# A two-layer decoder trunk: the last chunk before each FFN by token halves, ordered weight splits in the down projections, and buffers of their own for the z halves

## The chip, the core and the metric

The program runs on one core of one Trainium2 chip, whose engines work side by side, each through its own queue in order: PE does the matrix products, ACT (ScalarE) and DVE (VectorE) the element-wise work and the emptying of PSUM, POOL and SP issue transfers. The metric is the time of one execution in microseconds on the device. It is a median over a few runs.

## The reference

The trunk takes 1024 tokens of width 1024 through a gated short-convolution layer and an attention layer with a compressed K/V, each followed by a SwiGLU FFN of inner width 2816. All is float32. Cut to its core:

```
def swiglu_ffn(h, w13, w2):
    g, u = split(h @ w13, 2)
    return (silu(g) * u) @ w2
h = h + short_conv_mixer(rms_norm(h, g0), w_in, conv_w, w_out)   # (gate_b * conv(gate_c * val)) @ w_out
h = h + swiglu_ffn(rms_norm(h, g1), w13, w2)
k_nope, k_pe, v = shared_mla_kv(h, ...)
h = h + mla_mixer(rms_norm(h, g2), ..., w_o, k_nope, k_pe, v)    # causal attention, then @ w_o
h = h + swiglu_ffn(rms_norm(h, g3), w13, w2)
return rms_norm(h, g4)
```

## The kernel before

Activations lie transposed, 128 channels by 1024 tokens, and the tokens are handled as two halves T1 and T2 of 512. Every operand of a product, weight or activation, is split into a high part (a rounding cast on ACT, L95) and a low part (the rest, a subtraction on DVE, L96), and PE multiplies three times: high by high, high by low, low by high.

Most of the work runs in `pair` (L147 to L188). A pair of output blocks for two token halves and two halves of the inner dimension is made from seven products instead of eight (a Strassen form). The products are named "1" to "7" and run in the order SEQ = 1, 5, 6, 2, 7, 3, 4, but 1, 5, 6, 3, 7, 2, 4 (SEQ0) for the first pair of an FFN. Each has its own combination of weight blocks (made by DVE at L158 to L168, into a raw buffer `sums` or in place) and of activations (made by `operands`, L252). A product is 12 matmuls where the inner dimension has four chunks of 256. Products 1, 6, 7 and 4 add up in one and the same PSUM bank Z (`ps_z`), so each of these must wait until the value before it has been copied or added out; 5 and 3 add up in the bank Y (`ps_y`), and 2 has a bank beside it. In `blocks` (up projections and the conv input) the values after 1, 5 and 6 are copied by ACT into half tiles `z1`, `z5`, `z6` (L197), and DVE adds them to later products (L237). Six half tiles (tag "half", L73) serve z1, z5, z6, `u2` and the activation sums `t` together.

The FFN's down projection is `back` (L477 to L519). It takes the inner dimension in four groups of two, three, three and three chunks, and in each group four pairs of output blocks; a product is 6 matmuls in the first group, 9 in the others. Its results are collected in `h`: in the first group ACT copies four of the seven (L501) and DVE adds the others, later DVE adds all (L503). In the third group the residual stream is fetched again (`hs`, L515). Weights come through ten raw buffers (`wraw`) and five split buffers (`wop`).

Before each FFN stand the projections conv_out (`classic`, L213, two chunks of 128 channels at a time, 48 matmuls each) and w_o (`project_o`, L1017). When two chunks are done, `final` (L540) scales them by the gain on ACT (`xg`, L544), makes the seven activation operands, and queues the squares for the norm (`stats`, L296 on ACT, L297 on DVE). What stands in `queue` is put out between the products by `drip`.

The order in which each engine sees its instructions is decided by a scheduler at build time, from the order in the code and a modelled timeline; `sums` of a later pair can so come before evictions of an earlier one.

## Time and profile before

| | |
|---|---|
| runs | 2120.62, 2125.85, 2125.18 us; median 2125.18 us |
| profiled execution | 2121.5 us, its span 2119.7 us, mean granted TensorE clock 0.994 |
| PE | busy 2077.5 us (98% of the span), 9798 matmuls |
| PE's weight loads | 1730.1 us (82%) |
| DVE | 1627.7 us (77%), 2694 instructions |
| ACT | 935.5 us (44%) |
| POOL | 245.2 us (12%) |
| DMA | 321.28 MB, mean 152 GB/s |

Busy time of PE covers pipelined matmuls that overlap, so PE's idle stretches have to be looked for one by one. Times in rows of the trace count from the start of the span.

### The profile page before, as it was taken

The numbers are of one execution on the slowest core, as the hardware profiler recorded it, in microseconds if no ns is written. First come the engines' busy times: TensorE is split into PE (matmuls) and PEld (weight loads), VectorE is DVE, ScalarE is ACT, GpSimd is POOL, SyncE is SP. The second block draws the span as 40 slices with busy tenths as digits, with TensorE's granted clock in tenths as the row PEclk, the third lists the DMA queues.
The fourth block names the chain that finished last, engine by engine and source line by source line (L and its number), as shares of the span: only waits on it lengthen the run. The fifth ranks groups of instructions, "written<-read, shape, count | busy, mean of one in ns | idle before, by whom it ended". The sixth has DMA issues, their size and how long they took to land.

```text
span 2119.7 us, 27634 instructions
## 1 busy us (share of the span) xinstructions
PE 2077.5 (98%) x9798; PEld 1730.1 (82%) x9798; DVE 1627.7 (77%) x2694; ACT 935.5 (44%) x1729; POOL 245.2 (12%) x464
## 2 busy tenths in 40 slices
PE   8999999999999999999999999999999999999998
PEld 6878887888888878888888888887888888878886
DVE  5697757789988887689467767767888888887785
ACT  6633344444444453224345545445444444443235
POOL 1000100000101121110002022100001010121100
PEclk9999999999999999999999999999999999999998
DMA  6133462343545587865222124522445445685851
GB/s 246 35 96 119 145 208 92 122 147 127 179 139 168 178 305 236 272 220 156 62 52 68 38 63 124 170 82 85 128 134 175 141 159 154 199 285 195 292 186 80
DMA packets 266858, 321.28 MB, mean 152 GB/s; under 512 B 19343, under 2 KB 214096, under 8 KB 266720
## 3 DMA queue, kind: packets, MB, share of 16 engines
q0 software_dynamic: 61248, 201.46, 28.1%
q1 hardware_dynamic: 205472, 118.07, 19.0%
q8 instruction: 77, 1.26, 0.2%
q14 instruction: 61, 0.50, 0.1%
HBM read 206.22 MB, written 108.00 MB: 148 GB/s over the span
## 4 chain that ended last, share of the span: by engine, by line
PE 88%; DVE 6%; DMA 2%; ACT 2%; issue 2%; SPq 0%; POOL 0%; POOLq 0%; ACTq 0%; DVEq 0%
PE ps_z L183 35%; PE ps_y L183 26%; PE ps_c L228 7%; PE ps_s L947 4%; PE ps_wo L108 1%; PE ps_wo L110 1%; PE ps_wo L112 1%; PE ps_l L112 1%; PE ps_l L108 1%; PE ps_l L110 1%; PE ps_pv L985 1%; PE ps_pv L986 1%; DMA w<-in_conv_ffn_w_dram 1%; PE ps_pv L987 1%; PE ps_q L108 1%
## 5 line engine op out<-in xcount | busy, mean ns | idle before, releaser
L183 PE MATMUL ps_z<-x,wo 128*128 128x512 f32 x2532 | 608.7, 389 | 3.6 <-ACT z L197 2.8
L183 PEld LDWEIGHTS ps_z<-x,wo 128*128 128x128 f32 x2532 | 474.6, 188 | 104.4 <-ACT z L197 4.1
L183 PE MATMUL ps_y<-x,wo 128*128 128x512 f32 x1764 | 432.3, 389 | 1.2 <-DVE x L96 0.9
L183 PEld LDWEIGHTS ps_y<-x,wo 128*128 128x128 f32 x1764 | 330.5, 188 | 70.9 <-DVE x L96 1.8
L95 ACT CAST wo<-w 128x512 fp32r<-128x512 f32 (+2 forms) x423 | 238.7, 570 | 278.0 <-PE ps_z L183 109.0
L96 DVE TENSOR_TENSOR wo<-w,wo 128x512 fp32r<-128x512 f32 (+2 forms) x423 | 260.4, 622 | 61.9 <-ACT wo L95 61.0
L183 PE MATMUL ps_z<-xm,wo 128*128 128x512 f32 x960 | 239.0, 392 | 4.2 <-ACT wo L95 1.6
L183 PEld LDWEIGHTS ps_z<-xm,wo 128*128 128x128 f32 x960 | 178.6, 188 | 46.3 <-DVE h L503 3.4
L95 ACT CAST wo<-sums 128x512 fp32r<-128x512 f32 (+2 forms) x172 | 98.3, 572 | 256.7 <-PE ps_y L183 101.5
L183 PE MATMUL ps_y<-xm,wo 128*128 128x512 f32 x720 | 181.6, 390 | 2.0 <-DVE h L503 2.0
L88 POOL DMA_DIRECT2D md<-x x140 | 74.9, 536 | 737.8 <-DVE x L96 704.8
L183 PEld LDWEIGHTS ps_y<-xm,wo 128*128 128x128 f32 x720 | 134.7, 188 | 31.0 <-DVE h L503 2.9
L197 ACT COPY z<-ps_z 128x512 f32<-128x512 f32 x106 | 62.0, 585 | 136.6 <-PE ps_z L183 136.5
L96 DVE TENSOR_TENSOR wo<-sums,wo 128x512 fp32r<-128x512 f32 (+2 forms) x172 | 107.2, 623 | 14.3 <-ACT wo L95 12.7
L88 POOL DMA_DIRECT2D xm<-md x140 | 74.1, 535 | 251.3 <-PE ps_z L183 126.3
L503 DVE TENSOR_TENSOR h<-ps_z,h 128x512 f32<-128x512 f32 x104 | 71.4, 687 | 36.5 <-PE ps_z L183 35.7
L96 DVE TENSOR_TENSOR x<-t,x 128x512 fp32r<-128x512 f32 x136 | 92.0, 684 | 5.1 <-ACT x L95 5.1
L237 DVE TENSOR_TENSOR a<-ps_y,z 128x512 f32<-128x512 f32 x88 | 60.6, 688 | 42.4 <-PE ps_y L183 42.1
L95 ACT CAST x<-t 128x512 fp32r<-128x512 f32 x136 | 82.4, 621 | 20.9 <-DVE t L252 20.3
L953 ACT ACTIVATE p<-ps_s,mx,qscale 128x128 f32<-128x128 f32 (+3 forms) x64 | 53.4, 835 | 82.4 <-DVE mx L951 80.0
L158 DVE TENSOR_TENSOR sums<-w,w 128x512 f32<-128x512 f32 (+2 forms) x85 | 53.2, 626 | 29.4 <-DMA w<-in_mla_ffn_w_dram 13.4
L503 DVE TENSOR_TENSOR h<-ps_y,h 128x512 f32<-128x512 f32 x88 | 60.2, 685 | 19.9 <-PE ps_y L183 19.8
(297 smaller groups left out, 3344.8 us busy)
## 6 DMA issues: line engine op xcount, KB each, us to landing
md<-x POOLq DMA_DIRECT2D x140, 512.0 KB, 3.6
xm<-md POOLq DMA_DIRECT2D x140, 512.0 KB, 8.1
w<-in_conv_ffn_w_dram SPq DMA_DIRECT2D x88, 256.0 KB, 2.8
w<-in_mla_ffn_w_dram SPq DMA_DIRECT2D x88, 256.0 KB, 3.0
w<-in_conv_w_in_dram SPq DMA_DIRECT2D x48, 256.0 KB, 3.0
hd<-h POOLq DMA_DIRECT2D x24, 512.0 KB, 3.6
w<-in_conv_ffn_w_dram SPq DMA_DIRECT2D x48, 192.0 KB, 4.9
w<-in_mla_ffn_w_dram SPq DMA_DIRECT2D x48, 192.0 KB, 4.5
```

What stands on the lines that cost most here:

```text
L88: nc.gpsimd.dma_start(dst, src)
L95: nc.scalar.copy(out=hi, in_=src)
L96: (eng or nc.vector).tensor_tensor(lo, src, hi.bitcast(F32), ALU.subtract)
L108: nc.tensor.matmul(ps[:, hs], lhsT=wh, rhs=xh(k)[:, hs], start=st, stop=False)
L158: tt(sums, R["12"], R["22"], ALU.add)
L183: mm = lambda w_, x_, f: nc.tensor.matmul(b, lhsT=w_[:, m], rhs=x_, start=f, stop=True, skip_group_check=True)
L197: nc.scalar.copy(out=kept[name], in_=b)
L228: nc.tensor.matmul(ps[:, ts], lhsT=w_[:, m], rhs=X[i][f"b{kh}{th}"][:, q, :], start=st and j == 0, stop=en and j == 2)
L237: nc.vector.tensor_tensor(dst, ps, add, ALU.add)
L503: nc.vector.tensor_tensor(dst[name], b, dst[name], ALU.add)
L947: nc.tensor.matmul(ps[:, a:b], lhsT=q[:, qs], rhs=k[:, a:b], start=i == 0, stop=i == 4 and b < kw)
L953: nc.scalar.activation(p, ps[:, :kw], AF.Exp, bias=mx, scale=qscale[:, qb:qb + 1], accum_out=rsum)
```

## The change

Token halves. The last of the eight 128-channel chunks of conv_out, and of w_o, does all matmuls for T2 first and then all for T1, the same number as before. The new function `last` in `next_operands` takes the place of `final` for the last two chunks: step 1 scales the seventh chunk and queues operands 1 and 5 (which need that chunk alone), step 2, after T2, scales the half of the eighth chunk and queues operands 6, 3 and 7, step 3, after T1, the other half and operands 2 and 4. The squares of the last four chunks (LATE) are all queued behind step 3.

Ordered splits. In the down projection, the split and the weight sums of product N are issued, on each engine, after the evictions of the products N-7 to N-10 (`behind`, AHEAD = 7).

Shared sums. In the down projection's first group, where a weight block fills half a raw buffer, two pairs share one `sums` buffer.

Buffers. z1, z5 and z6 get three half tiles of their own (tag "z"); three remain for the others.

```diff
 EARLY = 2
+AHEAD = 7
+LATE = 4
...
     def half(name, dt=F32):
-        return slots.tile([P, HS], dt, name=name, tag="half", bufs=NHALF)
+        kind = "z" if name[0] == "z" else "half"
+        return slots.tile([P, HS], dt, name=name, tag=kind, bufs=NHALF // 2)
...
         return R
-    def pair(w, kps, X, c1, c2, hook, seq=SEQ):
+    marks = []
+    @contextmanager
+    def behind(n):
+        with ExitStack() as stack:
+            seen = set()
+            for insts in reversed(marks[:max(0, len(marks) - n + 1)][-4:]):
+                for e, inst in (insts or {}).items():
+                    if e not in seen:
+                        seen.add(e)
+                        stack.enter_context(tc.issue_after(inst.ins))
+            yield
+    def pair(w, kps, X, c1, c2, hook, seq=SEQ, sums=None, ahead=99):
         nk = len(X)
         n = nk * P
         R = {k: t[:, :n] for k, t in raw_blocks(w, kps, c1, c2).items()}
-        sums = wraw("sums")[:, :n]
+        if sums is None:
+            sums = wraw("sums")[:, :n]
...
             hi, lo = part(o, n)
-            split(hi, lo, source(name))
+            with behind(ahead):
+                split(hi, lo, source(name))
...
                 mm(lo, xh, False)
-            hook(name, b)
+            marks.append(hook(name, b))
...
             ps = ps2("ps_c")
-            for i in range(nk):
-                for kh in (1, 2):
-                    hi, lo = ops[kh - 1]
-                    m = slice(i * P, (i + 1) * P)
-                    st, en = i == 0 and kh == 1, i == nk - 1 and kh == 2
-                    for j, (w_, q) in enumerate(((hi, 0), (hi, 1), (lo, 0))):
-                        for th, ts in ((1, T1), (2, T2)):
-                            nc.tensor.matmul(ps[:, ts], lhsT=w_[:, m], rhs=X[i][f"b{kh}{th}"][:, q, :],
-                                             start=st and j == 0, stop=en and j == 2)
+            split_t = late and mi == 2
+            for ths in (((2, T2),), ((1, T1),)) if split_t else (((1, T1), (2, T2)),):
+                for i in range(nk):
+                    for kh in (1, 2):
+                        hi, lo = ops[kh - 1]
+                        m = slice(i * P, (i + 1) * P)
+                        st, en = i == 0 and kh == 1, i == nk - 1 and kh == 2
+                        for j, (w_, q) in enumerate(((hi, 0), (hi, 1), (lo, 0))):
+                            for th, ts in ths:
+                                nc.tensor.matmul(ps[:, ts], lhsT=w_[:, m], rhs=X[i][f"b{kh}{th}"][:, q, :],
+                                                 start=st and j == 0, stop=en and j == 2)
+                if split_t:
+                    emit(mi, ps, ths[0][1])
+            if split_t:
+                continue
             emit(mi, ps)
             drip(5)
...
                     if gi == 0 and name in "1654":
-                        nc.scalar.copy(out=dst[name], in_=b)
+                        done = {"a": nc.scalar.copy(out=dst[name], in_=b)}
                     else:
-                        nc.vector.tensor_tensor(dst[name], b, dst[name], ALU.add)
+                        done = {"v": nc.vector.tensor_tensor(dst[name], b, dst[name], ALU.add)}
                     if gi == len(GROUPS) - 1 and name == "3":
                         final(mp, 2)
-                pair(w2, g, ready, n1 * P, n2 * P, hook)
+                    return done
+                sums = None
+                if len(g) == 2:
+                    if mp % 2 == 0:
+                        both = wraw("sums")
+                    sums = (both[:, :HS // 2], both[:, HS // 2:])[mp % 2]
+                pair(w2, g, ready, n1 * P, n2 * P, hook, sums=sums, ahead=AHEAD)
...
         X = []
+        def scaled(x, n, ts=slice(0, S)):
+            nc.scalar.activation(x[:, ts], st[n][:, ts], AF.Copy, scale=gcol(gain, n))
         def final(mp):
             xs = []
             for n in (2 * mp, 2 * mp + 1):
                 if spill:
                     move(hd[n], st[n])
                 x = slot("xg")
-                nc.scalar.activation(x, st[n], AF.Copy, scale=gcol(gain, n))
+                scaled(x, n)
                 xs.append(x)
             X.append({})
             operands(*xs, X[mp].__setitem__)
             for n in (2 * mp, 2 * mp + 1):
-                queue.append(lambda n=n: stats(n, st[n]))
-            if mp == KD // 2 - 1:
-                drip(len(queue) - 2)
-        return X, final
+                if n < KD - LATE:
+                    queue.append(lambda n=n: stats(n, st[n]))
+        def last(step):
+            mp = KD // 2 - 1
+            n = 2 * mp + (step > 1)
+            if step == 1:
+                fin["x"] = [slot("xg"), slot("xg")]
+                scaled(fin["x"][0], n)
+                X.append({})
+                fin["put"] = operands(*fin["x"], X[mp].__setitem__, "15")
+            else:
+                scaled(fin["x"][1], n, T2 if step == 2 else T1)
+                fin["put"]("637" if step == 2 else "24")
+                drip()
+            if spill and step != 2:
+                move(hd[n], st[n])
+            if step == 3:
+                queue.extend(lambda n=n: stats(n, st[n]) for n in range(KD - LATE, KD))
+        fin = {}
+        return X, final, last
...
     st, h = stream()
-    X, final = next_operands(st, "conv_ffn_norm_g")
+    X, final, last = next_operands(st, "conv_ffn_norm_g")
     for mp in range(KD // 2):
-        def emit(mi, ps):
+        late = mp == KD // 2 - 1
+        def emit(mi, ps, ts=slice(0, S)):
             hn = h(2 * mp + mi - 1)
-            nc.vector.tensor_tensor(hn, ps, hn, ALU.add)
-        classic(w_out, Y, 2 * mp * P, (2 * mp + 1) * P, emit)
-        final(mp)
+            nc.vector.tensor_tensor(hn[:, ts], ps[:, ts], hn[:, ts], ALU.add)
+            if late:
+                last(1 if mi == 1 else 2 if ts == T2 else 3)
+        classic(w_out, Y, 2 * mp * P, (2 * mp + 1) * P, emit, late)
+        if not late:
+            final(mp)
...
     st, h_of = stream(move)
-    def project_o(O, k0, n):
+    def project_o(O, k0, n, late=None):
         ps = ps2("ps_wo")
+        if late:
+            parts = []
+            for a in range(0, len(O), 3):
+                ks = range(a, min(a + 3, len(O)))
+                parts.append((ks, wsplit("wo", w_o[:, k0 + a:k0 + ks[-1] + 1, n * P:(n + 1) * P], [P, len(ks), P])))
+            hn = h_of(n)
+            for step, ts in ((2, T2), (3, T1)):
+                for ks, w in parts:
+                    gemm(ps, lambda k: w(k - ks[0]), lambda k: O[k][0], lambda k: O[k][1], ks, ks[0] == 0,
+                         ks[-1] == len(O) - 1, halves=[ts])
+                nc.vector.tensor_tensor(hn[:, ts], ps[:, ts], hn[:, ts], ALU.add)
+                late(step)
+            return
...
         pv(*u)
-    X, final = next_operands(st, "mla_ffn_norm_g")
+    X, final, last = next_operands(st, "mla_ffn_norm_g")
     for n in range(KD):
-        project_o(O1, EARLY, n)
-        drip(5)
-        if n % 2:
+        project_o(O1, EARLY, n, last if n == KD - 1 else None)
+        if n < KD - 1:
+            drip(5)
+        if n % 2 and n < KD - 1:
             final(n // 2)
+        if n == KD - 2:
+            last(1)```

How instructions move, at three places. First ACT, around the end of conv_out: z_2834, z_2855 and z_2876 (in the change z_2830, z_2851, z_2872) are the copies of products 1, 5 and 6 of the FFN's first pair, the `wo` casts its weights. Before:

```order
L95 CAST x_2797<-xg 128x512
L95 CAST x_2802<-t_2800 128x512
L296 ACTIVATE sq<-h 128x1024
L197 COPY z_2834<-ps_z 128x512
L296 ACTIVATE sq<-h 128x1024
L95 CAST wo_2912<-w_2814 128x512
L197 COPY z_2855<-ps_y 128x512
L95 CAST wo_2928<-w_2812 128x512
L197 COPY z_2876<-ps_z 128x512
```

and with the change:

```order
L216 COPY z_2830<-ps_z 128x512
L98 CAST wo_2914<-w_2810 128x512
L566 ACTIVATE xg<-h,vec 128x512
L216 COPY z_2851<-ps_y 128x512
L98 CAST wo_2930<-w_2808 128x512
L98 CAST x_2792<-xg 128x512
L98 CAST x_2797<-t_2795 128x512
L317 ACTIVATE sq<-h 128x1024 x3
L216 COPY z_2872<-ps_z 128x512
```

The squares that stood around the copy of product 1 now stand, three in a row, between the copies of products 5 and 6; the scaling of the T1 half and two casts stand between those of 1 and 6 as well.

Second DVE, in the first group of the conv FFN's down projection, where w_6585 and w_6588 (w_6586 and w_6589 with the change) are weights of the group's last pair. Before:

```order
L503 TENSOR_TENSOR h<-ps_y,h 128x512
L96 TENSOR_TENSOR wo_6400<-w_6391,wo_6400 128x256
L96 TENSOR_TENSOR wo_6413<-sums,wo_6413 128x256
L158 TENSOR_TENSOR sums<-w_6585,w_6588 128x256
L503 TENSOR_TENSOR h<-ps_z,h 128x512
```

and with the change, at the later place to which that sum has moved:

```order
L524 TENSOR_TENSOR h<-ps_z,h 128x512
L182 TENSOR_TENSOR w_6494<-w_6494 128x256
L99 TENSOR_TENSOR wo_6523<-sums,wo_6523 128x256
L524 TENSOR_TENSOR h<-ps_y,h 128x512
L176 TENSOR_TENSOR sums<-w_6586,w_6589 128x256
L99 TENSOR_TENSOR wo_6534<-w_6497,wo_6534 128x256
```

The sum of the last pair stood ahead of evictions of the pair two before it; now it stands behind those of its own predecessor.

Third DVE, where the second group of the same projection goes over into the third: w_7258 and w_7260 are weights of the third group's second pair, wo_7149 (wo_7149 with the change too) the first product of its first pair. Before:

```order
L96 TENSOR_TENSOR wo_7107<-w_7018,wo_7107 128x384
L158 TENSOR_TENSOR sums<-w_7258,w_7260 128x384
L503 TENSOR_TENSOR h<-ps_z,h 128x512
L164 TENSOR_TENSOR w_7258<-w_7256,w_7258 128x384
L96 TENSOR_TENSOR wo_7149<-w_7138,wo_7149 128x384
```

and with the change:

```order
L524 TENSOR_TENSOR h<-ps_y,h 128x512
L176 TENSOR_TENSOR sums<-w_7140,w_7142 128x384
L99 TENSOR_TENSOR wo_7093<-w_7020,wo_7093 128x384
L99 TENSOR_TENSOR wo_7107<-w_7018,wo_7107 128x384
L524 TENSOR_TENSOR h<-ps_z,h 128x512
L99 TENSOR_TENSOR wo_7149<-w_7138,wo_7149 128x384
```

The sum of the second pair no longer stands ahead of the eviction of the pair before; in its place, some rows earlier, stands the sum of the first pair (w_7140, w_7142).

## Rows read from the trace of the kernel before

**Rows 1.** Page: the chain that ended last, by engine

```profile
PE 88%; DVE 6%; DMA 2%; ACT 2%; issue 2%; SPq 0%; POOL 0%; POOLq 0%; ACTq 0%; DVEq 0%
```

**Rows 2.** Waits of PE: us in total, times, longest

```profile
PE ps_z L183 <- ACT z L197: 2.8, 3, 1.2
PE ps_y L183 <- DVE h L503: 2.0, 2, 1.8
...
PE ps_z L183 <- DVE wo L96: 1.6, 3, 0.8
PE ps_z L183 <- ACT wo L95: 1.6, 2, 1.3
...
PE ps_z L183 <- DVE h L503: 1.4, 2, 0.8
...
PE ps_y L183 <- DVE x L96: 0.9, 2, 0.5
```

**Rows 3.** Timeline at conv_out's end: start, duration, engine, instruction, [idle before <-releaser]

```profile
355.96 1.14 ACT L95 CAST x<-t 128x512 fp32r<-128x512 f32 x2
...
358.00 1.29 DVE L96 TENSOR_TENSOR x<-t,x 128x512 fp32r<-128x512 f32 x2
...
359.08 1.05 ACT L296 ACTIVATE sq<-h 128x1024 f32<-128x1024 f32 x1
...
360.04 0.56 ACT L197 COPY z<-ps_z 128x512 f32<-128x512 f32 x1
...
360.51 1.06 ACT L296 ACTIVATE sq<-h 128x1024 f32<-128x1024 f32 x1
360.66 3.01 PE L183 MATMUL ps_z<-x,wo 128*128 128x512 f32 x12 [1.19 <-ACT z L197]
...
363.51 2.65 PE L183 MATMUL ps_y<-x,wo 128*128 128x512 f32 x11
363.71 0.59 ACT L197 COPY z<-ps_z 128x512 f32<-128x512 f32 x1 [0.63 <-PE ps_z L183]
```

**Rows 4.** Groups by line, 350 to 366 us: busy us, mean ns, idle before

```profile
L677 DVE TENSOR_TENSOR h<-ps_c,h 128x1024 f32<-128x1024 f32 x1 | 1.2, 1224 | 0.0
```

**Rows 5.** Timeline, first down group of the conv FFN

```profile
788.42 0.42 DVE L158 TENSOR_TENSOR sums<-w,w 128x256 f32<-128x256 f32 x1 [0.95 <-DMA w<-in_conv_ffn_w_dram]
...
793.01 0.72 PE L183 MATMUL ps_z<-xm,wo 128*128 128x512 f32 x2 [1.32 <-ACT wo L95]
```

**Rows 6.** Timeline, first down group of the MLA FFN

```profile
1886.63 0.42 DVE L158 TENSOR_TENSOR sums<-w,w 128x256 f32<-128x256 f32 x1 [1.23 <-DMA w<-in_mla_ffn_w_dram]
...
1887.71 1.66 PE L183 MATMUL ps_y<-xm,wo 128*128 128x512 f32 x6 [1.85 <-DVE h L503]
```

**Rows 7.** Timeline, second to third down group of the conv FFN

```profile
871.28 0.56 DVE L158 TENSOR_TENSOR sums<-w,w 128x384 f32<-128x384 f32 x1 [2.14 <-DMA w<-in_conv_ffn_w_dram]
...
872.50 1.65 PE L183 MATMUL ps_z<-xm,wo 128*128 128x512 f32 x6 [0.63 <-DVE h L503]
```

**Rows 8.** Timeline, the conv input projection

```profile
119.02 2.60 PE L183 MATMUL ps_z<-x,wo 128*128 128x512 f32 x10 [0.83 <-DVE wo L96]
...
123.12 0.62 ACT L95 CAST wo<-w 128x512 fp32r<-128x512 f32 x1 [5.22 <-DVE w L168]
...
124.28 1.45 PE L183 MATMUL ps_z<-x,wo 128*128 128x512 f32 x5 [0.40 <-ACT z L197]
```

**Rows 9.** Stretch: PE, PEld, DVE, ACT, POOL busy (instructions), clock, DMA share, GB/s

```profile
505.00:565.00 60.00, 59.78 (x264) 49.14 (x263) 60.00 (x86) 24.28 (x41) 4.67 (x9) 1.00 0.39 126
```

**Rows 10.** Timeline of SP's queue, third down group of the conv FFN

```profile
875.10 0.37 SPq L143 DMA_DIRECT2D w<-in_conv_ffn_w_dram  x1
...
881.45 1.24 SPq L515 DMA_DIRECT2D hs<-hd  x2
```

**Rows 11.** Weight loads of L143 issued 872 to 900 us

```profile
DMA to landing us min/median/max: 2.7/9.5/13.8
```

**Rows 12.** Timeline of PE, third down group, second pair to third

```profile
900.75 2.47 PE L183 MATMUL ps_z<-xm,wo 128*128 128x512 f32 x10
```

More of the change, by code (lines that the diff above doesn't have):

```diff
@@ L1 @@
 from collections import deque
-from contextlib import ExitStack
+from contextlib import ExitStack, contextmanager
 import numpy as np
@@ L99, in split, with gemm @@
             nc.vector.scalar_tensor_tensor(lo, src, gain, hi.bitcast(F32), ALU.mult, ALU.subtract)
-    def gemm(ps, w, xh, xl, kc, first=True, last=True, width=S):
-        halves = [slice(a, min(a + 512, width)) for a in range(0, width, 512)]
+    def gemm(ps, w, xh, xl, kc, first=True, last=True, width=S, halves=None):
+        halves = halves or [slice(a, min(a + 512, width)) for a in range(0, width, 512)]
         for i, k in enumerate(kc):
@@ L234, in take @@
         if add is None:
-            nc.scalar.copy(out=dst, in_=ps)
-        else:
-            nc.vector.tensor_tensor(dst, ps, add, ALU.add)
+            return {"a": nc.scalar.copy(out=dst, in_=ps)}
+        return {"v": nc.vector.tensor_tensor(dst, ps, add, ALU.add)}
     def op_split(name, src):
@@ L243, in op_split, with operands @@
         return o
-    def operands(u, v, put):
+    def operands(u, v, put, first=SEQ):
         b11, b12, b21, b22 = u[:, T1], u[:, T2], v[:, T1], v[:, T2]
@@ L604, in emit @@
         def emit(blk, ps, add):
-            take({"1": c, "2": v}[blk[0]][:, (T1, T2)[int(blk[1]) - 1]], ps, add)
+            return take({"1": c, "2": v}[blk[0]][:, (T1, T2)[int(blk[1]) - 1]], ps, add)
         first_product(w_in, (KD + j) * P, (2 * KD + j) * P, emit)
```

41 lines of the change are left out of this document (19 added, 22 removed).

## The prediction

> **What bounds the kernel now.** I read the chain of waits first. It runs through PE for 88% of the span, through DVE for 6% and through ACT and DMA for 2% each [rows 1]. The change removes no matmul: the halves of the last chunk hold 24 and 24 matmuls (18 and 18 for w_o) where 48 (36) stood. So the time can only change where PE stands idle, and the next view is the list of what PE waited for. Six of its entries belong to products of `pair`, the code that the change reaches. They hold 14 waits and 2.8 + 2.0 + 1.6 + 1.6 + 1.4 + 0.9 = 10.3 us [rows 2]. Attention has waits of its own; its instructions keep their order. A listed idle stretch is too short: eleven matmuls in a row take 2.65 us with a last one listed at 0.39, so one starts every (2.65 - 0.39)/10 = 0.226 us [rows 3] while it is listed as 0.39. Each stop hides 0.16 us more, and the 14 waits are worth 10.3 + 14 x 0.16 = 12.5 us. That is the most the change can gain, 0.6%. Last I read the timeline around each wait, to see which instruction was late and what stood ahead of it on its engine.
>
> **Token halves, at the end of conv_out and of w_o.** Before, PE stops twice at each: 0.45 us for the low part of an activation operand (two stops under DVE x, 0.9 us in all [rows 2]) and 1.19 us for the copy of product 1, which started only at 360.04 because a 1.05 us square had taken ACT at 359.08 [rows 3]. With the hidden part that is 1.64 + 0.32 = 2.0 us per boundary, 4.0 for both.
>
> With the change products 1 and 5 need only the seventh chunk, whose operands are made while PE works on the T2 half, and 18 of their 24 matmuls run between the two halves. The first stop goes. For the second I follow ACT in its new order from the end of the T1 half (time 0), with distances between starts from rows: cast (1.14 - 0.62) = 0.52 us, square 0.96 us (359.08 to 360.04), copy 0.47 us (360.04 to 360.51), and an engine takes a result about 0.04 us after its listed end (product 6 ends at 360.66 + 3.01 = 363.67, its copy starts at 363.71) [rows 3]. The 0.62 us for one cast is that of [rows 8]. Product 1 has four more matmuls in PE's row and ends, as listed, at 3 x 0.226 + 0.39 = 1.07. Its copy runs from 1.11 to 1.67, and product 6, due at 6 x 0.226 = 1.36, starts at about 1.7: a stop of 0.35 us. Behind that copy ACT does a cast, the scaling of the T1 half (no row has that; as the cast), the copy of product 5, a cast, two casts, three squares and then the copy of product 6: it starts at 1.11 + 0.47 + 0.52 + 0.52 + 0.47 + 0.52 + 1.04 + 2.88 = 7.5 and ends at 8.1. PE meanwhile needs 1.7 + 24 x 0.226 = 7.1 for products 6 and 3, and product 7 adds to the bank that this copy empties. It waits 0.95 us. So 2.0 us become 1.3, and the change gains 0.7 us per boundary, 1.4 us for both. Bounds: if the copy of product 6 is free in time, 1.65 us each; if the squares are each late by the 0.1 us that their listed length exceeds the distance, and the scaling as long as a square, nothing is left: 0 each; and if DVE, which makes the input of one of the casts, comes a subtraction late as well, -0.6 us each. I take the worked value, since ACT's order is fixed.
>
> Halving the last addition has a price of its own. Over 1024 tokens it took 1224 ns [rows 4], and two operations of half that width in a row take 1.29 us together [rows 3], so the price is at most 0.07 us. [...]
>
> The squares being later also makes the norm's scale later. It is needed first when the first pair's results are scaled, well behind product 4 of that pair, and no stop of PE stands there now. I put it at 0.
>
> **Ordered splits, second to third group.** DVE is in order, and a sum of the next pair's weights waited 2.14 us for its transfer with an eviction behind it that PE needed; PE stopped 0.63 us [rows 7]. The same pattern stands in the MLA FFN, and the two are the entry of 1.4 us [rows 2]. With the change that sum is issued behind the evictions. The sum that now stands near this place is that of the pair whose first product is about to run, and its weights landed long before. Gain: 1.4 + 2 x 0.16 = 1.7 us; bounds 0 and 1.7. Here I expect all of it; below 0 it can't go, as DVE gets no work there.
>
> **Ordered splits and shared sums, first group.** In the conv FFN a sum waited 0.95 us for its transfer [rows 5], in the MLA FFN 1.23 us [rows 6], each time ahead of evictions. PE stopped for 1.32 us a little later in the one [rows 5] and for 1.85 us at once in the other [rows 6]. With the change the last pair's sum is behind those evictions, and its transfer no longer has to wait for the first pair's `sums` buffer. What DVE saves is its idle time, not work: between those waits it is full. Another sum (0.42 us listed, about 0.33 us on DVE) moves forward into the chain that makes the last activation operands. So 0.95 - 0.33 = 0.6 us and 1.23 - 0.33 = 0.9 us come through to PE, 1.5 us together. Bounds: if DVE's backlog simply stays and the moved sum comes on top, -0.7 us; if all stops there go, the entries ACT wo (1.6), DVE h before Y (2.0) and DVE wo without the 0.83 us of the conv input (0.8) [rows 2], 4.4 + 6 x 0.16 = 5.4 us. I take the value near the low end because DVE's work there stays the same.
>
> **Conv input.** PE stops 0.83 us for a low part and 0.40 us for a copy that stood behind a cast, which itself waited for DVE [rows 8]. In the new order the first low part is ahead of a 1.22 us multiplication and the copy ahead of the cast, but a later split of the same pair falls back. Of 0.83 + 0.40 + 0.32 = 1.55 us I count half, 0.8 us; bounds -0.5 (the later split stops PE as long as the copy did) and 1.55.
>
> **Buffers.** Six half tiles become three and three; six shared ones were never the last thing a copy waited for in the rows above. I put this at 0, with 0.5 us either way.
>
> **The sum.** 1.4 + 1.7 + 1.5 + 0.8 = 5.4 us. The profiled execution of 2121.5 us becomes 2116.1 us. It lies 3.7 us below the median of the runs, 2125.18 us, whose three values spread over 5.2 us; off the median the forecast is 2119.8 us, a gain of 0.25%. A measurement of this kernel can't tell less than about 0.3%, 6.4 us, from no change.
>
> **Rivals.**
> A. All stops go. DVE gets ahead in the first groups and the copy of product 6 slips in before the squares hurt. The gain is the bound, 12.5 us: 2112.7 us. For it: every stop has one named instruction that the new order moves. Against it: three squares ahead of that copy, and no less work on a full DVE.
> B. The stops only move. The squares cost at each boundary what the halves gain, and the first groups stay as they were since DVE has the same work: only the second-to-third-group stops go, 1.7 us, 2123.5 us. For it: the ACT sum above comes within 0.7 us of this at each boundary.
> C. Slower: transfers. In the third group SP's queue now issues all four fetches of the residual stream ahead of the third pair's first weights. That weight was issued at 875.10, between them; now it comes behind the fetches issued from 881.45 on, which occupy the queue for 1.24 us [rows 10], about 882.5. Loads there take 9.5 us to land in the middle, 13.8 us at worst [rows 11], so it lands between 892.0 and 896.3. PE needs it, split, at 900.75 [rows 12], and a cast and a subtraction come before, 0.6 us each [rows 3]; with as much again for the queues of both engines PE needs it by 898.3. It is in time by 2 us at the least. If four full fetches in a row add more than 2 us to the worst landing, PE waits. At 3 us beyond, PE loses about 3 us at each of four such places (two in each FFN), 12 us, and with the gains the time is 2125.2 + 12 - 5.4 = 2131.8 us. [...]
> D. Slower, in the conv FFN's up projection. From 505 to 565 us DVE is busy 60.00 of 60 us [rows 9], since the rotary tables are made there. A split put one place later on a full DVE is late by 0.6 us, and 20 such places would eat the gain and 6.6 us more, 2131.8 us. Splits there have a microsecond or two to spare, so it needs several in one place.
>
> **Chances.** The forecast, gains between 3 and 8 us: 0.45. A: 0.2. B: 0.2. C: 0.1. D: 0.05. Faster by over 0.3% takes A and about two fifths of the forecast's case, with the spread of the runs: 0.40. Within 0.3% takes the rest of that case and B: 0.46. Slower takes C, most of D: 0.14. The range reaches from 2111 us, A with a fast set of runs, to 2127 us, B with a slow one. The likeliest case alone has 2117 to 2122 us.
>
> **What would show it.** In the profile after: PE's wait for low parts of x is gone at both boundaries, and two waits for ACT's copy stand in its place, about 0.2 us and 0.8 us as listed, with three squares on ACT between the copies of products 5 and 6. The waits under DVE h for Z are gone, and no sum of the second to third group waits on a transfer ahead of an eviction. In the first groups the sums' waits for DMA are gone while PE still stops for casts and evictions. If PE stops at the third pair of the third group, released by a split that a transfer released, C is right. If the first groups run through without a stop, I have taken DVE's backlog for more than it is.

## The result, and the profile after

The change made the kernel slower. Its median is 2127.34 us over 20 runs, and the kernel before, over 20 runs too, has 2122.69 us. The recorded ratio, here and below not quite the quotient of the medians (1.0022 here), is 1.0018, 95% interval 1.0010 to 1.0027. That is 2.1 to 5.7 us more, where the prediction had 5.4 us less. The profiled executions lie further apart: spans of 2126.3 and 2119.7 us, 6.6 us. Of all runs in this document one is left out, a run of the token halves alone that took 2596.24 us at a mean granted clock of 0.75.

The page after names PE as before, with 86% of the chain where it had 88%, and DVE with one more per cent [rows 1]:

```profile
PE 86%; DVE 7%; ACT 2%; DMA 2%; issue 2%; SPq 0%; POOL 0%; POOLq 0%; ACTq 0%; DVEq 0%
```

PE does the same work, so the difference is again in its stops. This is the list of what PE waited for, after, with total us, times and the longest; it answers to [rows 2]:

```profile
PE ps_z L202 <- DVE wo L99: 6.0, 5, 2.4
PE ps_y L202 <- issue: 3.2, 1, 3.2
...
PE ps_z L202 <- ACT z L216: 1.7, 3, 0.8
...
PE ps_y L202 <- ACT wo L98: 1.2, 1, 1.2
```

The low parts of x (0.9 us before) are gone, the waits for ACT's copy fell from 2.8 to 1.7 us and those for DVE h from 2.0 and 1.4 to under 1 each. All of that was predicted. But the wait for a low part of the weights rose from 1.6 to 6.0 us, one stop of 3.2 us, which the profile can't assign ("issue"), is new, and so is one of 1.2 us for a cast. These three entries are the loss, and the rest of this document is about them.

**The stops that were to go, went.** At conv_out's end, the timeline after (start, duration, engine, instruction, idle before and releaser) answers to [rows 3]:

```profile
358.14 3.06 PE L202 MATMUL ps_z<-x,wo 128*128 128x512 f32 x12 [0.23 <-ACT z L216]
...
361.15 2.96 ACT L317 ACTIVATE sq<-h 128x1024 f32<-128x1024 f32 x3
...
364.01 0.57 ACT L216 COPY z<-ps_z 128x512 f32<-128x512 f32 x1
...
364.63 1.65 PE L202 MATMUL ps_z<-x,wo 128*128 128x512 f32 x6 [0.72 <-ACT z L216]
```

Two short stops, three squares between the copies: 0.23 + 0.72 + 2 x 0.16 = 1.27 us for 2.0 before. At w_o's end it is 1.08 us. The halved addition itself, in the groups by line from 355 to 366 us (busy us, mean ns, idle before), took 691 ns, and the next DVE instruction starts 0.61 us after it, so two halves occupy 1.22 us, no more than the 1224 ns of the whole one [rows 4]:

```profile
L728 DVE TENSOR_TENSOR h<-ps_c,h 128x512 f32<-128x512 f32 x1 | 0.7, 691 | 0.2 <-PE ps_c L248 0.2
```

From the second to the third down group of the conv FFN, where PE stopped for 0.63 us behind a sum's transfer [rows 7], no stop is left. The sum now stands behind the evictions and waits for nothing:

```profile
872.85 0.84 PE L202 MATMUL ps_z<-x,wo 128*128 128x512 f32 x3
873.53 1.75 PE L202 MATMUL ps_z<-xm,wo 128*128 128x512 f32 x7
...
882.19 0.55 DVE L176 TENSOR_TENSOR sums<-w,w 128x384 f32<-128x384 f32 x1
```

In the first down group the last pair's sum waits no more either, and PE keeps four short stops, 1.40 us listed and 2.0 us with the hidden part; this answers to [rows 5]:

```profile
787.64 1.65 PE L202 MATMUL ps_y<-xm,wo 128*128 128x512 f32 x6 [0.43 <-DVE h L524]
...
792.45 0.41 DVE L176 TENSOR_TENSOR sums<-w,w 128x256 f32<-128x256 f32 x1
792.71 0.74 PE L202 MATMUL ps_z<-xm,wo 128*128 128x512 f32 x2 [0.24 <-ACT wo L98]
...
794.45 1.19 PE L202 MATMUL ps_z<-xm,wo 128*128 128x512 f32 x4 [0.55 <-DVE wo L99]
...
796.74 2.14 PE L202 MATMUL ps_z<-xm,wo 128*128 128x512 f32 x8 [0.18 <-ACT h L522]
```

The conv input's two stops [rows 8] became two others that the view lists, 0.30 us for a cast and, a dozen microseconds on, 0.53 us for the split that fell back:

```profile
125.93 0.73 PE L202 MATMUL ps_z<-xb,wo 128*128 128x512 f32 x2 [0.30 <-ACT wo L98]
...
137.71 0.50 PE L202 MATMUL ps_z<-x,wo 128*128 128x512 f32 x1 [0.53 <-DVE wo L99]
```

**New stop 1: the last pair of the up projection.** The timeline after, around 730 us in the conv FFN:

```profile
719.40 0.68 DVE L275 TENSOR_TENSOR t<-a,t 128x512 f32<-128x512 f32 x1
...
723.32 0.53 POOL L91 DMA_DIRECT2D md<-x  x1 [3.01 <-DVE x L99]
...
725.17 3.84 POOL L91 DMA_DIRECT2D xm<-md  x7
...
734.70 0.69 DVE L176 TENSOR_TENSOR sums<-w,w 128x512 f32<-128x512 f32 x1 [6.08 <-DMA w<-in_conv_ffn_w_dram]
735.30 0.68 DVE L99 TENSOR_TENSOR wo<-w,wo 128x512 fp32r<-128x512 f32 x1
...
736.04 2.33 PE L202 MATMUL ps_z<-x,wo 128*128 128x512 f32 x9 [2.01 <-DVE wo L99]
```

Read it from the bottom. PE waits for a split, the split stands behind a sum, the sum waits 6.08 us for its weights. Above that is what was under way meanwhile: POOL started seven loads of 512 KB at 725.17. In the kernel before POOL had them at 732.36:

```profile
728.52 0.69 DVE L252 TENSOR_TENSOR t<-a,t 128x512 f32<-128x512 f32 x1
...
731.83 0.53 POOL L88 DMA_DIRECT2D md<-x  x1 [9.99 <-DVE x L96]
732.36 3.80 POOL L88 DMA_DIRECT2D xm<-md  x7
```

The weights that SP issued from 724.4 to 729 us landed in this time in the kernel before (minimum, median, maximum):

```profile
DMA to landing us min/median/max: 2.8/2.8/2.9
```

and in the kernel after in this:

```profile
DMA to landing us min/median/max: 9.5/11.4/13.3
```

So loads that start 7 us earlier meet the last weights. They start earlier because POOL stores an operand ahead of them (`md<-x`), whose intermediate `t` lives in a half tile. When z and t shared six tiles, `t` was written at 728.52 us; with three tiles apart from z's it is written at 719.40, and the store goes out at 723.32 instead of 731.83. Ahead of the loads the last weights took 2.8 us at the median to land, beside them 11.4 us. The same stop stands in the MLA FFN at 1841.34, listed with 2.40 us.

**New stop 2: the fourth down group's first pair.** The timeline after:

```profile
941.27 1.22 DVE L543 TENSOR_TENSOR h<-h,hs 128x1024 f32<-128x1024 f32 x1 [4.72 <-DMA hs<-hd]
942.42 0.68 DVE L524 TENSOR_TENSOR h<-ps_z,h 128x512 f32<-128x512 f32 x1
943.02 0.68 DVE L524 TENSOR_TENSOR h<-ps_y,h 128x512 f32<-128x512 f32 x1
...
943.80 4.18 PE L202 MATMUL ps_y<-xm,wo 128*128 128x512 f32 x9 [3.24 <-issue]
```

An addition of a residual tile waits 4.72 us for its transfer, two evictions stand behind it, and PE goes on 0.1 us after the second (943.02 + 0.68 = 943.70). That is what "issue" hides here. Before, the same addition stood in the same place of DVE's order and waited 0.58 us:

```profile
939.08 1.23 DVE L516 TENSOR_TENSOR h<-h,hs 128x1024 f32<-128x1024 f32 x1 [0.58 <-DMA hs<-hd]
```

Two things meet. DVE, rid of its stalls, arrives at 941.27 - 4.72 = 936.55 instead of 938.50, and the pair of fetches takes 14.0 us at the least to land instead of 10.8. Why the fetches take longer is not shown: from 925 to 940 us the DMA share is 1.07 to 1.13 in both kernels. In the MLA FFN the same addition waits 2.63 us and PE stops for 1.16 us there.

**The clock.** After this stop the granted clock was 0.50 from 943.16 to 949.99 us, with PE busy but for the end of the stop; after stop 1 it stayed at 1.00. The stretches after (busy us of PE, PEld, DVE, ACT and POOL with their instructions, then clock, DMA share, GB/s):

```profile
736.00:739.00 3.00, 2.96 (x13) 2.46 (x14) 3.00 (x6) 0.00 (x0) 0.31 (x1) 1.00 1.13 388
943.16:949.99 6.83, 6.19 (x15) 4.92 (x16) 5.86 (x10) 0.51 (x1) 0.00 (x0) 0.50 0.11 31
```

The 15 matmuls there start 0.427 us apart and not 0.227: 3.0 us more.

**The balance.** With 0.16 us added to each listed stop, as in the prediction, the gains are 1.65 us (boundaries), 1.9 (first groups, 0.8 and 1.1), 1.7 (second to third group) and 0.4 (conv input), 5.65 us in all. The losses are 2.17 + 2.56 (stop 1), 3.40 + 3.0 (stop 2 in the conv FFN with its clock), 1.32 + 0.47 in the MLA FFN, and two small new stops of 0.26 and 0.33 us: 13.5 us. The net is 7.9 us, where the spans differ by 6.6. Both kernels have the same number of matmuls, so the starts of PE's matmuls can be compared one by one, and these say where the count by listed stops is off: the change is 0.6 us ahead at the kernel's start, which it doesn't touch, a short stop before at 988 us is gone, and from 99 to 155 us, in the conv input, the gain is 0.05 us and not 0.4, since short stops that no view lists are new there. The medians differ by less, 4.65 us; I have one profile of each, so how often the clock falls after stop 2 is not known.

### The profile page after: what moved, and what is told of

Its sections match the earlier page's. It is cut to its first block, busy times and chain, and to the rows that moved or that the text cites. A ratio compares the mean times of both kernels' runs of the same rounds, so it can differ in the third digit from the quotient of the medians.

```text
span 2126.3 us, 27708 instructions
## 1 busy us (share of the span) xinstructions
PE 2080.7 (98%) x9798; PEld 1732.9 (81%) x9798; DVE 1621.8 (76%) x2696; ACT 936.5 (44%) x1731; POOL 244.9 (12%) x464
## 4 chain that ended last, share of the span: by engine, by line
PE 86%; DVE 7%; ACT 2%; DMA 2%; issue 2%; SPq 0%; POOL 0%; POOLq 0%; ACTq 0%; DVEq 0%
PE ps_z L202 35%; PE ps_y L202 26%; PE ps_c L248 7%; PE ps_s L1000 4%; PE ps_wo L111 1%; PE ps_wo L113 1%; PE ps_wo L115 1%; PE ps_l L115 1%; PE ps_l L111 1%; PE ps_l L113 1%; DVE wo L99 1%; PE ps_pv L1038 1%; PE ps_pv L1039 1%; PE ps_pv L1040 1%; PE ps_q L111 1%
## 5 line engine op out<-in xcount | busy, mean ns | idle before, releaser
L202 PE MATMUL ps_z<-x,wo 128*128 128x512 f32 x2532 | 609.1, 389 | 6.6 <-DVE wo L99 4.9
L202 PEld LDWEIGHTS ps_z<-x,wo 128*128 128x128 f32 x2532 | 474.7, 188 | 108.3 <-DVE wo L99 6.6
L202 PE MATMUL ps_y<-x,wo 128*128 128x512 f32 x1764 | 432.5, 389 | 0.2 <-ACT z L216 0.2
L202 PEld LDWEIGHTS ps_y<-x,wo 128*128 128x128 f32 x1764 | 330.7, 188 | 69.2 <-ACT z L216 0.6
L98 ACT CAST wo<-w 128x512 fp32r<-128x512 f32 (+2 forms) x423 | 238.7, 570 | 317.7 <-PE ps_y L202 126.1
L99 DVE TENSOR_TENSOR wo<-w,wo 128x512 fp32r<-128x512 f32 (+2 forms) x423 | 259.7, 622 | 33.6 <-ACT wo L98 32.7
L202 PE MATMUL ps_z<-xm,wo 128*128 128x512 f32 x960 | 241.1, 392 | 2.3 <-DVE wo L99 1.1
L98 ACT CAST wo<-sums 128x512 fp32r<-128x512 f32 (+2 forms) x172 | 98.4, 572 | 278.5 <-PE ps_y L202 113.0
L202 PEld LDWEIGHTS ps_z<-xm,wo 128*128 128x128 f32 x960 | 179.8, 189 | 43.4 <-DVE wo L99 2.0
L202 PE MATMUL ps_y<-xm,wo 128*128 128x512 f32 x720 | 185.2, 394 | 5.5 <-issue 3.2
L202 PEld LDWEIGHTS ps_y<-xm,wo 128*128 128x128 f32 x720 | 135.7, 189 | 36.1 <-issue 3.6
L91 POOL DMA_DIRECT2D md<-x x140 | 74.4, 532 | 726.5 <-DVE x L99 704.6
L216 ACT COPY z<-ps_z 128x512 f32<-128x512 f32 x106 | 62.0, 584 | 126.6 <-PE ps_z L202 126.2
L99 DVE TENSOR_TENSOR wo<-sums,wo 128x512 fp32r<-128x512 f32 (+2 forms) x172 | 107.2, 623 | 12.7 <-ACT wo L98 12.1
L260 DVE TENSOR_TENSOR a<-ps_y,z 128x512 f32<-128x512 f32 x88 | 60.5, 688 | 64.1 <-PE ps_y L202 63.9
L91 POOL DMA_DIRECT2D xm<-md x140 | 74.1, 535 | 260.2 <-PE ps_z L202 156.5
L524 DVE TENSOR_TENSOR h<-ps_z,h 128x512 f32<-128x512 f32 x104 | 71.6, 688 | 40.1 <-PE ps_z L202 39.6
L98 ACT CAST x<-t 128x512 fp32r<-128x512 f32 x136 | 82.8, 620 | 30.3 <-DVE t L275 23.4
L99 DVE TENSOR_TENSOR x<-t,x 128x512 fp32r<-128x512 f32 x136 | 91.9, 684 | 2.6 <-ACT x L98 2.4
L524 DVE TENSOR_TENSOR h<-ps_y,h 128x512 f32<-128x512 f32 x88 | 60.4, 686 | 38.9 <-PE ps_y L202 38.9
L176 DVE TENSOR_TENSOR sums<-w,w 128x512 f32<-128x512 f32 (+2 forms) x85 | 53.1, 624 | 35.1 <-DMA w<-in_mla_ffn_w_dram 13.8
```

The lines of the kernel that those rows point to most:

```text
L91: nc.gpsimd.dma_start(dst, src)
L98: nc.scalar.copy(out=hi, in_=src)
L99: (eng or nc.vector).tensor_tensor(lo, src, hi.bitcast(F32), ALU.subtract)
L176: tt(sums, R["12"], R["22"], ALU.add)
L202: mm = lambda w_, x_, f: nc.tensor.matmul(b, lhsT=w_[:, m], rhs=x_, start=f, stop=True, skip_group_check=True)
L216: return {"a": nc.scalar.copy(out=kept[name], in_=b)}
```

## Experiments

In the expectations, as recorded, each theory carries its number. In words: the reason that I held is that z's own buffers make stop 1 by way of POOL's queue and that the ordered splits make stop 2. Each ratio is to the kernel before on the same chip, whose medians were 2122.9 (first four), 2123.34 (next four) and 2123.43 us (last two).

**Change without z's own buffers.**

```
-        kind = "z" if name[0] == "z" else "half"
-        return slots.tile([P, HS], dt, name=name, tag=kind, bufs=NHALF // 2)
+        return slots.tile([P, HS], dt, name=name, tag="half", bufs=NHALF)
```

> The changed kernel with one edit undone: z1, z5, z6 share the six half tiles again. Theory 1 (the z tiles' own buffers let the activation sum t4 of an FFN's last stored operands be made about 9 us earlier, its store goes out earlier, the seven 512 KB loads queued behind that store on POOL start 7 us earlier and run into the weight loads of the last up pair): PE's stops of 2.0 us at 736 us and 2.4 us at 1841 us, released by a weight split behind a sum that waits 6 us for its transfer, are gone; the time falls by about 4.7 us to 2122.6 us, a ratio to the kernel before of 1.000. The stop at 941 us stays. Theory 2 (the loads start earlier only because PE runs ahead after the halved chunk): both stops stay, the ratio stays at 1.002.

Measured: 2125.51 us, ratio 1.0011 (1.0002 to 1.0019). Stop 1 is gone from both FFNs; PE runs through the stretch:

```profile
733.00:740.00 7.00, 7.00 (x33) 5.79 (x32) 5.50 (x10) 1.87 (x3) 3.86 (x8) 1.00 1.04 338
```

Yet by the medians only 1.8 us come back, and the intervals of the two ratios overlap. The boundary loses what it had gained:

```profile
359.64 0.58 ACT L215 COPY z<-ps_z 128x512 f32<-128x512 f32 x1
...
360.26 3.02 PE L201 MATMUL ps_z<-x,wo 128*128 128x512 f32 x12 [2.21 <-ACT z L215]
```

With shared tiles the copy of product 1 stands in ACT's program behind the scaling and three casts for the operands: one stop of 2.21 + 0.16 = 2.37 us, worse than the 2.0 before, and 2.33 at w_o. The conv input goes back to 0.99 and 0.60 us. So the z buffers cause stop 1 and are also what the token halves need.

**Change without the order of the splits.**

```
-                pair(w2, g, ready, n1 * P, n2 * P, hook, sums=sums, ahead=AHEAD)
+                pair(w2, g, ready, n1 * P, n2 * P, hook, sums=sums)
```

> The changed kernel without the ordered splits (the shared sums, the halves and the z buffers stay). Theory 1 (issuing the sums late makes SP fetch the residual stream in blocks ahead of weights in the third down group, so that the last residual tile lands after DVE has reached its addition): PE's stop of 3.2 us at 941 us, the 15 matmuls at half clock behind it (3 us) and the 1.2 us at 2045 us are gone, the two stops at the change from the second to the third down group come back (1.7 us) and those of the first group grow by 1 to 2 us; the stops at 736 and 1841 us stay; about 2122 us, ratio 1.000. Theory 2 (the residual tile lands late because the whole stretch runs earlier against the activation loads, whatever the order of the splits): the stop at 941 us stays, the ratio rises to 1.003.

Measured: 2143.56 us, ratio 1.0095 (1.0081 to 1.0108). The stops near 941 and 2045 are gone, as expected of the reason held, and those from the second to the third group are back (0.75 and 1.30 us). What I had not expected are 8.6 us in each FFN at the first group:

```profile
783.53 0.42 DVE L176 TENSOR_TENSOR sums<-w,w 128x256 f32<-128x256 f32 x1 [10.66 <-DMA w<-in_conv_ffn_w_dram]
783.87 0.68 DVE L260 TENSOR_TENSOR a<-ps_y,z 128x512 f32<-128x512 f32 x1
...
784.61 4.61 PE L202 MATMUL ps_y<-x,wo 128*128 128x512 f32 x12 [8.40 <-DVE a L260]
```

Without the order, a sum that no longer waits for the `sums` buffer runs ahead of an eviction and waits 10.66 us for its weights there. That a shared buffer let the sum go ahead is argued and not shown alone: z's own buffers by themselves, the next run, bring a smaller stop of the same kind with sums unshared. With both parts the order is needed.

**Z's own buffers alone.** The kernel before with the first edit turned round (`-` and `+` exchanged).

> The kernel before with one part of the change alone: z tiles get three buffers of their own, three remain for the others. Theory 1 (early t4, early loads): the two stops at the last up pair of each FFN appear, 2.0 to 2.6 us each, and the time rises by about 4.7 us, ratio 1.002. Theory 2 (they need the other parts of the change): no new stop, ratio 1.000.

Measured: 2133.3 us, ratio 1.0045 (1.0030 to 1.0059), the largest loss of a part by itself:

```profile
735.16 0.69 DVE L159 TENSOR_TENSOR sums<-w,w 128x512 f32<-128x512 f32 x1 [7.43 <-DMA w<-in_conv_ffn_w_dram]
...
736.51 1.74 PE L184 MATMUL ps_z<-x,wo 128*128 128x512 f32 x5 [3.35 <-DVE wo L97]
```

Stop 1 is 3.51 us here with the hidden part, and 2.79 in the MLA FFN. The first groups stop for 4.57 and 3.13 us as well, which I had not expected: a sum of the last pair's weights comes ahead of evictions there and waits 3.86 and 2.43 us for its transfer. The clock is at 0.50 for a while after three of the four. It costs 10 us by itself.

At the two boundaries, though, z's own buffers do alone what the halves were meant to do, and more:

```profile
357.62 0.58 ACT L198 COPY z<-ps_z 128x512 f32<-128x512 f32 x1
...
358.25 3.02 PE L184 MATMUL ps_z<-x,wo 128*128 128x512 f32 x12 [0.33 <-ACT z L198]
...
360.14 2.01 ACT L297 ACTIVATE sq<-h 128x1024 f32<-128x1024 f32 x2
```

The copy of product 1 now stands ahead of both squares, and PE's only listed stop is 0.33 us, at w_o's end too: 0.49 us with the hidden part, where the kernel before has 2.0 and the change 1.27 and 1.08. The conv input's stops of 0.30 and 0.54 us are those of the change as well.

**Token halves alone.** The change, without z's own buffers and without order and shared sums.

```
-                pair(w2, g, ready, n1 * P, n2 * P, hook, sums=sums, ahead=AHEAD)
+                pair(w2, g, ready, n1 * P, n2 * P, hook, sums=None)
```

> The kernel before with one part of the change alone: the last chunk of conv_out and w_o by token halves, with the later squares. Theory 1 (the prediction's sum for this part held): at both boundaries PE's 2.0 us become two stops worth 1.1 to 1.3 us, the second behind three squares on ACT; the gain is 1.5 us, ratio 0.9993, which these runs can hardly tell from 1. Theory 2 (halving costs as much elsewhere): ratio 1.000 or above, with new stops up to 60 us behind either boundary.

Measured: 2124.21 us, ratio 1.0006 (0.9998 to 1.0015), no difference that can be told. The boundaries stop PE for 2.37 and 2.33 us, against 2.0 before. The halves gain nothing without z's tiles, and beside them they cost: 0.49 us without halves, 1.27 and 1.08 with them.

**Ordered splits and shared sums alone.** The change, without z's own buffers and without the halves.

```
-LATE = 4
+LATE = 0
...
-        late = mp == KD // 2 - 1
+        late = False
```

> The kernel before with one part of the change alone: ordered splits and shared sums in the down projections. Theory 1 (this part brings both the gain in the down groups and the late residual tile): the two stops from the second to the third group are gone (1.7 us), the first groups gain 1 to 2 us, and a stop of 2.5 to 3.5 us appears near 937 us, released late by the addition of a residual tile, and one of 1 to 2 us at its counterpart in the MLA FFN; with up to 3 us of half clock behind the first, the time lies between 1 us below and 5 us above the kernel before, ratio 1.001. Theory 2 (the late residual tile needs the earlier arrival of the whole stretch that the other parts bring): no such stop, ratio 0.9985.

Measured: 2125.39 us, ratio 1.0009 (0.9999 to 1.0018). The gains in the down groups are there, and stop 2 with them: 2.17 us at 942 with the clock at 0.50 after it, 1.91 us at 2044. The two about cancel. In this execution the clock also fell to 0.50 at conv_out's end, which this kernel has as the kernel before.

**Change with late additions.** Each residual addition is held behind an eviction, and the last two of each FFN are queued three products later.

```
+                    if mp == KD // 2 - 1:
+                        queue.extend([lambda: None] * 3)
...
+                            with behind(1):
+                                nc.vector.tensor_tensor(st[m], st[m], t, ALU.add)
...
-                drip()
+                if gi != len(GROUPS) - 2:
+                    drip()
```

> The changed kernel with the additions of the residual stream's last two tiles in each FFN put behind four evictions of the next group's first pair. Theory 1 (PE stops at 941 us because DVE, in order, waits in that addition for a tile that lands late while two evictions stand behind it): the stops at 941 us (3.4 us), the half clock behind it (3.0 us) and the stops at 2045 us (1.8 us) are gone; about 8 us below the changed kernel, 2119 us, ratio 0.998. Theory 2 (the transfers as such are late, and the weights of the next pairs as well): DVE waits in a weight sum or PE for a split instead, and less than half of the 8 us is won.

Measured: 2121.12 us, ratio 0.9986 (0.9977 to 0.9994). By the medians that is 6.2 us less than the change; stop 2 counts 3.40 + 3.0 us in the conv FFN with its clock and 1.8 us in the MLA FFN, and all of it is gone. The addition comes behind its evictions and waits for nothing:

```profile
942.63 0.69 DVE L524 TENSOR_TENSOR h<-ps_y,h 128x512 f32<-128x512 f32 x1 [0.78 <-PE ps_y L202]
943.24 1.22 DVE L548 TENSOR_TENSOR h<-h,hs 128x1024 f32<-128x1024 f32 x1
```

Its fetch landed 12.6 us after its issue, 1.4 us sooner than in the change, but well after the time at which DVE had come to the addition there; now no eviction stands behind it. Stop 1 stays, 2.05 and 2.18 us.

**Change with late loads.** The seven loads are issued one step of the up projection later.

```
-            if j == order[-3]:
+            if j == order[-2]:
                 for name in SEQ:
                     ready[0][name] = load(GROUPS[0][0], name)
```

> The changed kernel with the seven activation loads of the first down group issued behind two more stores, those of the FFN's last up pairs. Theory 1 (the loads, started 7 us earlier than before, take the DMA engines from the weights of the last up pair): the weights land before DVE gets to their sum, the stops at 736 and 1841 us are gone, about 4.7 us below the changed kernel, 2122.6 us, ratio 1.000. Theory 2 (the sum of that pair now stands one place ahead of the split that PE waits for, and this alone makes the stop): the stops stay, shorter than 1 us at the least. If the loads come too late for the first down group, a new stop of several us stands near 777 us.

Measured: 2123.7 us, ratio 1.0000 (0.9991 to 1.0010). This edit touches neither the buffers nor DVE's program, and stop 1 is gone from both FFNs:

```profile
730.71 0.69 DVE L176 TENSOR_TENSOR sums<-w,w 128x512 f32<-128x512 f32 x1 [1.76 <-DMA w<-in_conv_ffn_w_dram]
731.04 4.24 PE L202 MATMUL ps_z<-x,wo 128*128 128x512 f32 x18
```

That shows the loads to be the link. Now they are the late ones: the first down group waits for them, 0.65 and 0.63 us, and for an eviction, 1.21 us; in the MLA FFN 2.28 us with the clock at 0.50. Part of the gain is given back. Not all of the 3.6 us by which the median lies below the change's belongs to stop 1: stop 2 was 1.05 and 1.52 us in this execution, without half clock.

**Change with three repairs.** Late additions, late loads, and the squares of the last four chunks three products later.

```
             if step == 3:
+                queue.extend([lambda: None] * 3)
                 queue.extend(lambda n=n: stats(n, st[n]) for n in range(KD - LATE, KD))
```

> The changed kernel with three repairs: the late additions, the late loads, and the squares of the last four chunks queued three products later, so that ACT's copy of product 6 stands ahead of them. If the causes are as told and don't meet each other: 8 us, 4.7 us and about 1.8 us (the stops before product 7 at both boundaries, 0.9 us each, gone) below the changed kernel, about 2113 us, ratio to the kernel before 0.9955. If each repair only moves transfers into the next wait, no more than a third of it: ratio 1.000.

Measured: 2114.1 us, ratio 0.9955 (0.9941 to 0.9970): 9.2 us faster than the kernel before and 13.2 faster than the change, as expected. No half clock between the kernel's start and its last 20 us, as in the profile before. With the squares later the stop at conv_out's end is 0.38 us, where z's own buffers alone left 0.49. Left are, in the first down group, a wait for the late loads and this one:

```profile
784.58 1.66 PE L202 MATMUL ps_z<-xm,wo 128*128 128x512 f32 x6 [1.41 <-ACT h L522]
```

**Three repairs, two loads early and five late.**

```
-            if j == order[-2]:
-                for name in SEQ:
+            if j in order[-3:-1]:
+                for name in SEQ[:2] if j == order[-3] else SEQ[2:]:
```

> The three repairs, with the seven activation loads of the first down group in two parts: two at the early place, five behind two more stores. Theory 1 (seven loads in a row are what delays the last up pair's weights, and five late ones still come in time for the first down group): no stop at 736 and 1841 us, the stops of 0.6 and 1.6 us near 780 us shrink by half or more; 2112 us, ratio 0.995. Theory 2 (any load that starts early delays those weights, any late one comes late): both kinds of stop, each shorter; 2114 us, no better than the three repairs.

Measured: 2114.1 us, ratio 0.9953 (0.9939 to 0.9966), the same as all seven late. Two early loads bring stop 1 back, though in the conv FFN alone; there the store of a rotary table is issued just ahead of them:

```profile
722.48 0.53 POOL L91 DMA_DIRECT2D trig<-sin  x1 [0.79 <-DVE sin L487]
723.00 1.08 POOL L91 DMA_DIRECT2D xm<-md  x2
...
732.72 0.69 DVE L176 TENSOR_TENSOR sums<-w,w 128x512 f32<-128x512 f32 x1 [6.28 <-DMA w<-in_conv_ffn_w_dram]
...
734.07 1.21 PE L202 MATMUL ps_z<-x,wo 128*128 128x512 f32 x4 [2.20 <-DVE wo L99]
```

In the MLA FFN they cost nothing. The first group of the conv FFN stops in four pieces, 2.4 us in all, the longest 1.49; with seven late there are two, 2.2 us in all. Neither of the quoted readings fits both FFNs.

**Three repairs, four loads early and three late.** As the last, with `SEQ[:4]` and `SEQ[4:]`.

> As the kernel before it, with four loads early and three late. Theory 1: the stops near 780 us are gone, and the weights of the last up pair land one to two loads' time (1.5 us each) later than with two: a stop of 0 to 1 us at 736 us; 2111 to 2113 us, ratio 0.995. Theory 2: the stop at 736 us is back at over 1 us in both FFNs, 2115 us or more.

Measured: 2121.09 us, ratio 0.9985 (0.9976 to 0.9994). Stop 1 is in both FFNs, 1.96 and 2.84 us, with the clock at 0.50 after the longer one, and in the conv FFN its sum waits 5.88 us. So four early loads are enough to bring it to both: the second of the quoted theories. The first one's 1.5 us for a load is near an estimate from the stretch of 733 to 740 us quoted above: 512 KB at its 338 GB/s take 1.55 us.

## Why the prediction was wrong

**The step that failed is "Buffers".** It put the split of six half tiles into three and three at 0, with 0.5 us either way, on the ground that a tile was never the last thing that a copy waited for. That looked at what a copy waited for in the old order, and at z's side alone. On z's side the order itself changed: with tiles of its own the copy of product 1 goes ahead of the squares, which by itself takes 1.5 us off each boundary. The tiles of `t` were waited for, and with tiles apart from z's `t` comes 9 us earlier at the end of the up projection. The step asked which wait goes, and not what the freed instruction releases: here a store on POOL and seven loads behind it in the same queue. On t's side this term measured 4.7 us of loss as part of the change; by itself the whole edit costs 10 us. The wait of POOL's queue for DVE was in the trace, 9.99 us ahead of that store, and I hadn't read POOL's queue at all.

**"Ordered splits" had the gain right and missed a second wait.** The 1.7 us came as worked out. But the step said that below 0 it can't go, since DVE gets no work there. DVE got no work; it came 2 us earlier to an addition whose transfer came 2.2 us later, and that one stands ahead of evictions too. Rival C had the fetches of the residual stream and the right place in SP's queue, but looked at the weights behind them, for a split in the third group. The late one was the fetch itself, in the fourth group's first pair. C's price of 12 us is of the order of the 8 us that stop 2 cost in both FFNs with its clock, but that is luck, as it is not C's mechanism; C's own stop, at the third pair of the third group, didn't come.

**The clock was in no term.** The 3.0 us after stop 2 are a term that the sum didn't have.

**"Token halves" had the number right and the cause wrong.** 1.65 us against 1.4; the two stops at conv_out's end are 0.23 and 0.72 us listed, about 0.2 and 0.8 forecast, with the three squares where the sum had put them. The working assumed that the copy of product 1 finds a tile at once. That holds only with z's own tiles, which the prediction had priced at nothing. The four kernels that have or lack the two parts settle it: with neither PE stops for 2.0 us at a boundary, with the halves alone for 2.37 and 2.33, with z's tiles alone for 0.49, with both for 1.27 and 1.08. The gain is that of the tiles, and the halves give 0.6 to 0.8 us of it back. Halving the addition as such, which the prediction priced at 0.07 us at most and left out of its sum, shows no loss: two halves at 0.61 us from start to start make 1.22 us, the whole one took 1224 ns.

**First groups:** 1.9 us against 1.5, 0.8 and 1.1 for 0.6 and 0.9. They stop for casts and evictions still, as said. **Conv input:** 0.4 us by the listed stops, 0.05 by the starts of the matmuls, against 0.8; the later split that falls back stops PE for 0.69 us at 137 us. Here too it is the z buffers that move the stops.

**The bound** of 12.5 us left out two entries of `pair` that the list also has, `PE ps_z L183 <- ACT h L501: 0.4, 2, 0.2` and `PE ps_y L183 <- ACT z L197: 0.2, 1, 0.2`; with them it is 13.6 us. Nothing turned on it.

So the gains summed to 5.65 us where 5.4 were forecast. That they lie so near is partly luck: the boundaries' gain came from a part put at 0, and the first groups' surplus stands against what the conv input lacks. The sum was wrong by what it had put at nothing or left out, 13.5 us of new stops.

## What to carry to other kernels

When a change frees an instruction earlier, follow what it releases down to the queues: each DMA issued behind it can start earlier too, as the seven loads did here by 7 us, and the question is which transfer it then meets. Splitting a shared pool is never only a matter of the tile that was waited for, since the wait that goes may have held back something useful to hold back; once it goes, place the transfers by hand, as the late loads did. And read for each engine, after the change, which wait for a transfer now stands ahead of an eviction in its order, for that engine may come to it earlier, as DVE did here by 2 us. Where a change has several parts, run each alone too: here one part brought the gain that the prediction gave to another.

## What the runs showed of the hardware

**The clock after a stop.** In these profiles a granted clock of 0.50 followed some stops of PE and not others of about the same length. In the change it followed the stop of 3.40 us and neither of 2.17 and 2.56. In the kernel with the token halves alone it followed the stop of 2.37 us at conv_out's end and not the one of 2.33 us at w_o's. With ordered splits and shared sums alone it followed two shorter ones at conv_out's end, 0.63 us and, after two matmuls, 1.35 us; in the profile of the kernel before the same two were followed by 1.00. After stop 2 of the change each matmul at 0.50 started 0.2 us later, 0.427 us behind the one ahead of it and not 0.227. It was 15 of them there, 3.0 us, and 8 behind the same stop in the change without z's own buffers, where the stop was 2.73 us: 1.6 us on top of it.

**Landing times.** 256 KB of weights landed in 2.8 us with the loads of 512 KB behind them, and in 9.5 to 13.3 us with seven of those started in the same microseconds. The kernel with three repairs issues one store of 512 KB in that stretch and none of the loads, and its weights had these times:

```profile
DMA to landing us min/median/max: 4.4/4.9/5.4
```
